# More pairs of half-wide products in the ConvFFN, none in the short convolution

## The chip, the cores and the metric

The kernel runs on one core of one Trainium2 chip. The metric is the device time of one execution in microseconds; before the change the median of three runs is 1096.01 us (1095.03 to 1096.32).

## The reference

A trunk of two layers on 512 positions of 1024 channels, all in float32. Layer 0 mixes positions by gated linear attention in chunks of 64 with 4 heads, layer 1 by a short gated convolution; each mixer is followed by a causal ConvFFN, and each of the four blocks reads an RMS norm of x and adds its result to x. A last norm ends it.

```
x = x + mixer(rmsnorm(x))                   # layer 0: GLA;  layer 1: y = b * conv3(c * u), then y @ w_out
up = conv3(rmsnorm(x) @ w_up)               # causal, depthwise, width 3; 2 x 2816 columns
a, u = up[..., :2816], up[..., 2816:]
x = x + (silu(a) * u) @ w_down
```

## The kernel before, in words

**Layout and precision.** Channels lie on the 128 partitions and the 512 positions on the free axis, so x is 8 tiles x[0..7] of 128 x 512. Every float32 product is made of three matmuls: each operand is split into a high half in the format that TensorE multiplies and a low half with the remainder, and high x high, high x low and low x high are added up in PSUM (`mm3`, L282). The norm's gain goes into these halves of x (`norm_parts`, L307 and L308), its row factor r is multiplied in after the product.

**Weights.** All weights are read once, as a list of units of up to 128 x 1024, in the order in which they are used (class `Weights`). A unit is loaded on SyncE's queue into one of 6 raw buffers, then split into halves in one of 4 buffers (L127 on ScalarE for the high half). The low half comes from VectorE (L132: raw minus high), or, for a unit that is marked `added`, from ScalarE, which writes the negated high half (L129), and a DMA on GpSimd's queue that adds the raw values to it (L130). `take()` hands out one unit and prepares the third unit after it. Before the change only the units of w_down are marked.

**ConvFFN.** It has 22 columns of 128 channels; column j has an a tile and a u tile, two units of w_up. They are worked through in four blocks of 6, 5, 5 and 6 columns; between the columns of a block stand the down products (`dn`) of the block before, which add into x. `ff_steps` writes this order out. A column of the plain kind is a step `up`: two groups of 24 matmuls with 512 columns. A column in `SEVEN` is a pair of the other kind: the two tiles, the two halves of the 8 channel tiles and the two halves of the positions make a 2 x 2 by 2 x 2 block product, which is done with seven half-size products instead of eight (`product`, L605; 12 matmuls of 256 columns each), in steps `s1` (four products) and `s2` (three). For it the raw weights of the two tiles are added and subtracted on VectorE (`forms`, L141 to L148), and the x parts likewise once per ConvFFN (`seven_forms`, L589 to L595): four sets, k = 0..3, each from x[k] and x[k + 4], made after columns 1 to 4. The results are joined by quarter-size operations (L626 to L642), and then every column goes through the convolution, silu, the gating product and a split into halves g (L297, L298).

**Short convolution.** Eight times three whole groups (c, u and b, 24 matmuls each), a convolution between, then 8 groups `so` that add into x.

**Order.** The program text gives priorities; a scheduler at compile time places each instruction on its engine's queue by when it expects it to be ready, and the queues run in that order. The row norm's sum of squares (L318, L319) is split (L324, L325) between the first and the second group after a residual and summed on TensorE after the second (`inv_rms_rows`).

Of the kernel before, what the change touches and what calls it, by code (L numbers as in the profile page):

```python
# [10 lines left out]
F32 = mybir.dt.float32  # L11
F32R = mybir.dt.float32r
AF = mybir.ActivationFunctionType
ALU = mybir.AluOpType
# [13 lines left out]
WARM = 10  # L28
BLOCKS = ((0, 6), (6, 11), (11, 16), (16, 22))
HALVED = 4  # L30
SEVEN = (6, 7, 8, 9, 10, 11, 12, 13, 14, 15, 16, 17, 18, 20, 21)


@with_exitstack
def trunk_kernel(ctx, tc, xT, w_qk, w_v, w_g, w_up_gate, b_gate, w_go, w_sc, w_so, w_up, w_dn,
# [15 lines left out]
    def wk(name, shape=(P, T), dt=F32, bufs=2, tag=None, pool=work):  # L51
        return pool.tile(list(shape), dt, tag=tag or name, name=name, bufs=bufs)
# [141 lines left out]
            return self.split.pop(self.ng - 1)  # L194

    W = Weights()
    for src in ([w_qk[i] for i in range(8)] + [w_v[i] for i in range(8)] + [w_g[i] for i in range(8)]
                + [w_go[i] for i in range(8)]):
# [24 lines left out]

    add_ffn(0)
    for src in [w_sc[i] for i in range(3 * KD)] + [w_so[i] for i in range(KD)]:
        W.add(src)
    add_ffn(1)
    take = W.take

# [336 lines left out]
    gate_tile(6)  # L566
    gate_tile(7)

    def residual(src, gi):
        for m in range(KD):  # L570
            V.tensor_add(x[m], x[m], src(m))
            norm_parts(m, gi)
            norm_squares(m)


    go, w = [ps("go0"), ps("go1")], [take(), take()]
# [3 lines left out]
                mm3(go[m], w[m][k], yparts[k], k == 0, k == KD - 1)  # L580
    residual(lambda m: go[m] if m < 2 else group(f"go{m}", yparts), 1)


    def seven_forms(k, gi, y, neg):


        lo, hi = slice(0, HT), slice(HT, T)
        g1, g2 = col(gi, k), col(gi, k + 4)
        S.activation(y[:, lo], x[k][:, hi], AF.Copy, scale=g1)  # L589
        S.activation(y[:, hi], x[k + 4][:, hi], AF.Copy, scale=g2)  # L590
        ta, tb = wk("ta", tag="sq"), wk("tb", tag="sq")
        V.scalar_tensor_tensor(ta[:, lo], x[k][:, lo], g1, y[:, lo], op0=ALU.mult, op1=ALU.subtract)
        V.tensor_sub(tb[:, lo], y[:, lo], y[:, hi])
# [4 lines left out]
        return [tuple(p[:, c] for p in t) for t in (a, b) for c in (lo, hi)]  # L598

    def product(out, ws, xs, first):  # L600
        for k in range(4):
# [12 lines left out]
    def cut(ks, c):  # L614
        return [tuple(p[:, c] for p in xparts[k]) for k in ks]

    def seven_first(tf):
# [5 lines left out]
        us = [wk("u", bufs=3) for _ in range(2)]  # L623
# [6 lines left out]
        S.copy(us[0][:, lo], ab[:, hi])  # L630
        V.tensor_add(us[0][:, lo], us[0][:, lo], ab[:, lo])
        return dc, ab, e, us

    def seven_last(dc, ab, e, us, tf):
# [4 lines left out]
        S.copy(us[0][:, hi], ab[:, lo])  # L639
        V.tensor_sub(us[1][:, lo], dc[:, lo], us[0][:, hi])  # L640
        V.tensor_sub(us[1][:, hi], e, us[0][:, hi])
        V.tensor_add(us[0][:, hi], dc[:, hi], us[0][:, hi])  # L642
        return us

    def ffn_blocks(l, gi, gnext):
        gp, r, tf = {}, None, [[], [], [], []]
        neg = tk("neg", (P, KD), bufs=1)
        V.tensor_scalar_mul(neg, vec[:, gi * KD:(gi + 1) * KD], -1.0)
        for st in ff_steps():
            if st[0] == "dn":  # L650
                _, b, m = st
                if gnext is None and b == len(BLOCKS) - 1 and m == HALVED:
                    break
                part = group(f"dn{m}", [gp[j] for j in range(*BLOCKS[b])])
                V.tensor_add(x[m], x[m], part)  # L655
                if b == len(BLOCKS) - 1:
                    if gnext is not None:
                        norm_parts(m, gnext)
                    norm_squares(m)
                continue  # L660
            j = st[1]
            if st[0] == "s1":
                begun = seven_first(tf)
                continue
            if st[0] == "s2":
                us = seven_last(*begun, tf)
                for u in us:
                    V.tensor_mul(u, u, r)  # L668
            else:
                ups = [group("up0", xparts)]  # L670
                if j == 0:
                    sums = sum_parts(acc[0])
                ups.append(group("up1", xparts))
                if j == 0:
                    r = inv_rms_rows(sums, D)
                    y = wk("y", tag="acc", bufs=1)
                us = [wk("u", bufs=3) for _ in range(2)]
                for u, up in zip(us, ups):
                    V.tensor_mul(u, up, r)
            cs = [conv3(us[i], ffcw[:, l, i * NFF + j, :], f"c{i}") for i in range(2)]  # L680
            S.activation(cs[0], cs[0], AF.Silu)  # L681
            V.tensor_mul(cs[1], cs[1], cs[0])
            gp[j] = split_to(cs[1], f"g{j}", f"b{j % 11}")
            if len(SEVEN) and 1 <= j <= 4:
                for t, f in zip(tf, seven_forms(j - 1, gi, y, neg)):
                    t.append(f)
        return [gp[j] for j in range(*BLOCKS[-1])]

    HT = T // 2
    ffn_blocks(0, 1, 2)  # L690


    yparts = []
    for i in range(KD):
        cp = group("scc", xparts)
        if i == 0:
            sums = sum_parts(acc[0])
        up = group("scu", xparts)
        if i == 0:
            r = inv_rms_rows(sums, D)  # L700
        cr = wk("u", bufs=3)
        V.tensor_mul(cr, cp, r)
        ur = wk("u", bufs=3)
        V.tensor_mul(ur, up, r)
        V.tensor_mul(ur, ur, cr)
        cv = conv3(ur, sccw[:, i, :], "c0")
        V.tensor_mul(cv, cv, r)
        bp = group("scb", xparts)
# [5 lines left out]
    gp = ffn_blocks(1, 3, None)  # L714

    wlast = {m: take() for m in range(HALVED, KD)}

# [133 lines left out]
```

## Time and profile before

| | |
|---|---|
| profiled execution | 1095.35 us |
| its span, first to last instruction | 1093.6 us |
| median of three runs | 1096.01 us |
| granted TensorE clock, mean over the span | 0.997 |
| ScalarE busy | 593.1 us, 54% |
| GpSimd busy | 60.4 us, 6% |
| chain that ended last | TensorE 98%, DMA 1% |

A busy time is the time in which an engine executes something. Matmuls are pipelined, so one may be counted as running while the next has begun, and the mean duration of one is longer than the distance from its start to the start of the next. The chain of waits is followed back from the last instruction, at each step to what released it or to the instruction before it on its engine; in order of time it reads as the path that sets the end.

### The profile page before, as it was taken

The page shows a single profiled execution, that of the slowest core. Times are in us where ns is not written, and L with a number is a line of the kernel's source. Part 1 is how long each engine was busy: PE and PEld are TensorE (multiplying, and loading weights), DVE is VectorE, ACT ScalarE, POOL GpSimd, SP SyncE. Part 2 cuts the span into 40 slices and gives each one's busy share as a digit, 9 for nine tenths or more (in the row PEclk, how much of TensorE's full clock was granted, in tenths as well). Part 3 has the DMA queues.
Part 4 walks back from the last instruction along what each step waited for, and adds up shares of the span by engine and source line. Part 5 has one row for each costly group of instructions (what it writes and reads, how often), then busy time and mean ns, then how long its engine had stood idle before and what let it go on. Part 6 is the DMA issues. An engine that isn't in the chain of part 4 may idle for free.

```text
span 1093.6 us, 15686 instructions
## 1 busy us (share of the span) xinstructions
PE 1083.8 (99%) x6106; PEld 953.0 (87%) x6106; DVE 842.9 (77%) x1267; ACT 593.1 (54%) x902; POOL 60.4 (6%) x82
## 2 busy tenths in 40 slices
PE   9999999999999999999999999999999999999997
PEld 7888888888999999989888888888899999999986
DVE  8874676589889899897566555568988989899754
ACT  7565764466555565556642222345655655655563
POOL 1000000000000000001200000000000000000020
PEclk9999999999999999999999999999999999999998
DMA  8332123321545545355853333332254654545473
GB/s 290 109 93 81 58 78 97 96 92 54 150 126 145 138 133 137 107 150 125 204 170 92 102 89 104 97 100 68 82 140 108 161 139 121 139 126 150 116 149 93
DMA packets 44719, 131.42 MB, mean 120 GB/s; under 512 B 4898, under 2 KB 7714, under 8 KB 44644
## 3 DMA queue, kind: packets, MB, share of 16 engines
q1 hardware_dynamic: 35428, 107.34, 31.3%
q0 software_dynamic: 9216, 23.07, 11.7%
q8 instruction: 47, 0.77, 0.3%
q14 instruction: 28, 0.23, 0.1%
HBM read 105.23 MB, written 2.10 MB: 98 GB/s over the span
## 4 chain that ended last, share of the span: by engine, by line
PE 98%; DMA 1%; ACT 0%; DVE 0%; issue 0%; SPq 0%; DVEq 0%
PE dn L282 21%; PE updc L605 16%; PE up L282 14%; PE upab L605 12%; PE g L282 4%; PE v L282 4%; PE so L282 4%; PE scb L282 4%; PE scu L282 4%; PE scc L282 4%; PE go L282 4%; PE k L282 2%; PE q L282 2%; PE dnl L282 1%; PE o L504 1%; PE o L506 0%
## 5 line engine op out<-in xcount | busy, mean ns | idle before, releaser
L127 ACT CAST wh<-wr 128x1024 fp32r<-128x1024 f32 (+4 forms) x280 | 247.0, 884 | 339.7 <-PE upab L605 78.7
L132 DVE TENSOR_TENSOR wl<-wr,wh 128x1024 fp32r<-128x1024 f32 (+2 forms) x216 | 225.6, 1052 | 67.9 <-ACT wh L127 67.5
L130 POOL DMA_DIRECT2D wl<-wr x64 | 55.4, 866 | 977.2 <-ACT wl L129 725.7
L282 PE MATMUL up<-xh,wh 128*128 128x512 f32 x224 | 87.1, 389 | 0.0
L282 PE MATMUL up<-xl,wh 128*128 128x512 f32 x224 | 87.1, 389 | 0.0
L282 PE MATMUL up<-xh,wl 128*128 128x512 f32 x224 | 87.1, 389 | 0.0
L341 ACT ACTIVATE c<-u,ffcw 128x512 f32<-128x512 f32 x88 | 59.8, 716 | 32.2 <-DVE u L668 19.2
L605 PE MATMUL upab<-xh,wh 128*128 128x256 f32 x240 | 67.9, 283 | 0.0
L605 PE MATMUL upab<-xl,wh 128*128 128x256 f32 x240 | 67.9, 283 | 0.0
L605 PE MATMUL upab<-xh,wl 128*128 128x256 f32 x240 | 67.9, 283 | 0.0
L342 DVE SCALAR_TENSOR_TENSOR c<-u,ffcw,c 128x511 f32<-128x511 f32 x88 | 62.8, 745 | 6.0 <-ACT c L341 6.0
L343 DVE SCALAR_TENSOR_TENSOR c<-u,ffcw,c 128x510 f32<-128x510 f32 x88 | 62.6, 743 | 0.1
L129 ACT ACTIVATE wl<-wh 128x768 fp32r<-128x768 f32 (+1 forms) x64 | 50.8, 794 | 0.9
L282 PEld LDWEIGHTS up<-xh,wl 128*128 128x128 f32 x224 | 42.0, 188 | 8.8
L282 PEld LDWEIGHTS up<-xh,wh 128*128 128x128 f32 x224 | 42.0, 188 | 8.8
L282 PEld LDWEIGHTS up<-xl,wh 128*128 128x128 f32 x224 | 42.0, 188 | 8.6
L655 DVE TENSOR_TENSOR x<-x,dn 128x512 f32<-128x512 f32 x60 | 40.9, 682 | 10.8 <-PE dn L282 10.4
L605 PEld LDWEIGHTS upab<-xh,wh 128*128 128x128 f32 x240 | 46.1, 192 | 0.0
L605 PEld LDWEIGHTS upab<-xl,wh 128*128 128x128 f32 x240 | 46.1, 192 | 0.0
L605 PEld LDWEIGHTS upab<-xh,wl 128*128 128x128 f32 x240 | 46.1, 192 | 0.0
L681 ACT ACTIVATE c<-c 128x512 f32<-128x512 f32 x44 | 27.8, 632 | 29.9 <-DVE c L343 29.9
L668 DVE TENSOR_TENSOR u<-u,r 128x512 f32<-128x512 f32 x60 | 38.5, 683 | 0.0
(682 smaller groups left out, 3210.3 us busy)
## 6 DMA issues: line engine op xcount, KB each, us to landing
wr<-in_w_up SPq DMA_DIRECT2D x88, 512.0 KB, 3.6
wr<-in_w_dn SPq DMA_DIRECT2D x32, 384.0 KB, 3.4
wl<-wr POOLq DMA_DIRECT2D x32, 384.0 KB, 4.4
wr<-in_w_sc SPq DMA_DIRECT2D x24, 512.0 KB, 3.6
wr<-in_w_dn SPq DMA_DIRECT2D x32, 320.0 KB, 2.9
wl<-wr POOLq DMA_DIRECT2D x32, 320.0 KB, 3.8
wr<-in_w_v SPq DMA_DIRECT2D x8, 512.0 KB, 3.6
wr<-in_w_g SPq DMA_DIRECT2D x8, 512.0 KB, 3.7
```

Source lines behind the costliest of these rows:

```text
L127: S.copy(hh, src)
L129: S.activation(ll, hh.bitcast(F32), AF.Copy, scale=-1.0)
L130: G.dma_start(ll, src, accum_op=ALU.add)
L132: V.tensor_sub(ll, src, hh.bitcast(F32))
L282: PE.matmul(out, lhsT=a, rhs=b, start=first and i == 0, stop=last and i == 2)
L341: S.activation(c, u, AF.Copy, scale=cw[:, 2:3])
L342: V.scalar_tensor_tensor(c[:, 1:], u[:, :T - 1], cw[:, 1:2], c[:, 1:], op0=ALU.mult, op1=ALU.add)
L343: V.scalar_tensor_tensor(c[:, 2:], u[:, :T - 2], cw[:, 0:1], c[:, 2:], op0=ALU.mult, op1=ALU.add)
L605: PE.matmul(out, lhsT=a, rhs=b, start=first and k == 0 and i == 0, stop=k == 3 and i == 2, skip_group_check=not first)
L655: V.tensor_add(x[m], x[m], part)
L668: V.tensor_mul(u, u, r)
L681: S.activation(cs[0], cs[0], AF.Silu)
```

## The change

- The list `SEVEN` goes. In both ConvFFNs the columns 3, 5 and 6 to 21 are pairs of the other kind; 0, 1, 2 and 4 stay whole. Block 0 runs as up 0, up 1, s1 3, first tile of 2 (`ua`), s2 3, s1 5, second tile of 2 (`ub`), s2 5, up 4.
- The sets of x parts are made in the residual before a block (`settle`): k = 0 with x[5], k = 1 with x[6], k = 2 and 3 with x[7]; also in the one before the short convolution. They have temporary buffers of their own (tags b12h, b12l, b13l).
- More units are marked `added`: the whole units of w_up, all of w_sc, and the second half of w_go and w_so. So are the halves of gated tiles except columns 4, 10, 15, 20 and 21 (`SOON`) and of the first six y parts of the short convolution.
- The short convolution could take pairs of c and u (`SC_SEVEN`); that list is empty, so all its groups stay whole. It multiplies c by the square of r instead of c and u by r each.
- `seven_first` and `seven_last` allocate the second result tile later.

```diff
-SEVEN = (6, 7, 8, 9, 10, 11, 12, 13, 14, 15, 16, 17, 18, 20, 21)
+SOON = (4, 10, 15, 20, 21)
+SC_SEVEN = ()
...
+    for m in range(KD):
+        W.add(w_go[m], m >= KD // 2)
...
-        steps = [("up", j) for j in range(*BLOCKS[0])]
+        steps = [("up", 0), ("up", 1), ("s1", 3), ("ua", 2), ("s2", 3), ("s1", 5), ("ub", 2), ("s2", 5), ("up", 4)]
...
-                steps += [("s1", j), dn[0], ("s2", j)] + dn[1:] if j in SEVEN else [("up", j)] + dn
+                steps += [("s1", j), dn[0], ("s2", j)] + dn[1:]
...
-                W.add(w_up[l, 2 * st[1]])
-                W.add(w_up[l, 2 * st[1] + 1])
+                for i in {"up": (0, 1), "ua": (0,), "ub": (1,)}[st[0]]:
+                    W.add(w_up[l, 2 * st[1] + i], True)
...
-    def split_to(src, name, tag):
+    def split_to(src, name, tag, added=False):
...
-        S.copy(h, src)
-        V.tensor_sub(l, src, h.bitcast(F32))
+        W.halve(h, l, src, added)
...
-        ta, tb = wk("ta", tag="sq"), wk("tb", tag="sq")
+        ta, tb = bt("b12h", f"ta{gi}{k}"), bt("b12l", f"tb{gi}{k}")
...
+    def settle(m, part, gi):
+
+        V.tensor_add(x[m], x[m], part)
+        norm_parts(m, gi)
+        norm_squares(m)
+        if m == 0:
+            settle.neg, settle.y = tk("neg", (P, KD), bufs=1), bt("b13l", f"y{gi}")
+            V.tensor_scalar_mul(settle.neg, vec[:, gi * KD:(gi + 1) * KD], -1.0)
+            for t in tf:
+                del t[:]
+        for k in {5: (0,), 6: (1,), 7: (2, 3)}.get(m, ()):
+            for t, f in zip(tf, seven_forms(k, gi, settle.y, settle.neg)):
+                t.append(f)
...
+        def gate(j):
+            a, u = cs.pop((j, 0)), cs.pop((j, 1))
+            S.activation(a, a, AF.Silu)
+            V.tensor_mul(u, u, a)
+            gp[j] = split_to(u, f"g{j}", f"b{j % 11}", j not in SOON)
...
+                r2 = bt("b10h", "r2s")
+                V.tensor_mul(r2, r, r)
+            cr, ur = wk("u", bufs=3), wk("u", bufs=3)
+            V.tensor_mul(cr, cp, r2)
+            V.tensor_mul(ur, up, cr)
...
-        yparts.append(split_to(cv, f"s{i}", f"b{i}"))
+        yparts.append(split_to(cv, f"s{i}", f"b{i}", i < KD - 2))
```

## Rows read from the trace of the kernel before

**Rows 1.** The page's busy shares: engine, us, share of the span, instructions.
```profile
PE 1083.8 (99%) x6106; PEld 953.0 (87%) x6106; DVE 842.9 (77%) x1267; ACT 593.1 (54%) x902; POOL 60.4 (6%) x82
```

**Rows 2.** The chain of waits in order of time: start us, length us, what.
```profile
210.82 10.88 PE up L282 x48
...
276.55 2.87 PE updc L605 x24
279.42 2.88 PE upab L605 x24
282.30 4.11 PE dn L282 x18
286.41 2.87 PE updc L605 x24
289.28 1.44 PE upab L605 x12
```

**Rows 3.** The costliest groups of TensorE: count, busy us, mean ns, idle before.
```profile
L282 PE MATMUL up<-xh,wh 128*128 128x512 f32 x224 | 87.1, 389 | 0.0
...
L605 PE MATMUL upab<-xh,wh 128*128 128x256 f32 x240 | 67.9, 283 | 0.0
```

**Rows 4.** Busy us by stage, layer 0: ConvFFN block 0, block 2, block 3.
```profile
210.65:276.55 65.90, 65.90 (x293) 54.59 (x292) 59.53 (x89) 40.79 (x60) 1.01 (x1) 1.00 0.25 74
359.75:437.51 77.76, 77.76 (x542) 72.90 (x542) 71.17 (x118) 45.36 (x76) 6.89 (x8) 1.00 0.51 137
437.51:526.10 88.59, 88.59 (x589) 81.88 (x589) 73.16 (x118) 50.92 (x82) 8.63 (x10) 1.00 0.52 135
```
Columns after the stretch: its length, TensorE, its weight loads, VectorE, ScalarE, GpSimd, granted clock, DMA share, GB/s.

**Rows 5.** Groups of instructions by shape on VectorE and ScalarE.
```profile
L132 DVE TENSOR_TENSOR wl<-wr,wh 128x1024 fp32r<-128x1024 f32 x150 | 182.9, 1220 | 64.4 <-ACT wh L127 64.1
L132 DVE TENSOR_TENSOR wl<-wr,wh 128x512 fp32r<-128x512 f32 x62 | 42.4, 685 | 2.8 <-ACT wh L127 2.8
L592 DVE SCALAR_TENSOR_TENSOR ta<-x,small,y 128x256 f32<-128x256 f32 x8 | 3.8, 475 | 6.5 <-PE sums L332 6.5
...
L127 ACT CAST wh<-wr 128x1024 fp32r<-128x1024 f32 x150 | 157.3, 1049 | 242.2 <-issue 49.3 <-PE upab L605 41.5 <-PE scu L282 32.1
L127 ACT CAST wh<-wr 128x512 fp32r<-128x512 f32 x62 | 38.2, 619 | 12.4 <-DVE wr L143 5.1 <-DMA wr<-in_w_up 4.5 <-PE updc L605 2.5
L129 ACT ACTIVATE wl<-wh 128x768 fp32r<-128x768 f32 x32 | 27.1, 847 | 0.5
```

**Rows 6.** The page's DMA issues, accumulating ones: count, KB each, us to landing.
```profile
wl<-wr POOLq DMA_DIRECT2D x32, 384.0 KB, 4.4
...
wl<-wr POOLq DMA_DIRECT2D x32, 320.0 KB, 3.8
```

**Rows 7.** The page's DMA queues: packets, MB, share of 16 engines over the span.
```profile
q1 hardware_dynamic: 35428, 107.34, 31.3%
q0 software_dynamic: 9216, 23.07, 11.7%
```

**Rows 8.** DMA queues and issues from 526 to 559 us, block 3's down products.
```profile
q1 hardware_dynamic: 1323, 4.72, 41.0%
q0 software_dynamic: 864, 2.36, 38.7%
...
wl<-wr POOLq DMA_DIRECT2D x5, 384.0 KB, 5.6
```

**Rows 9.** Order of time on ScalarE and GpSimd, there: start, length, instruction.
```profile
539.20 0.85 ACT L129 ACTIVATE wl<-wh 128x768 fp32r<-128x768 f32 x1
...
538.80 0.86 POOL L130 DMA_DIRECT2D wl<-wr  x1 [2.89 <-ACT wl L129]
540.40 0.88 POOL L130 DMA_DIRECT2D wl<-wr  x1 [0.73 <-ACT wl L129]
```

**Rows 10.** VectorE after the last group of w_go: low half of the squares.
```profile
214.89 0.69 DVE L325 TENSOR_TENSOR sl<-acc,sh 128x512 fp32r<-128x512 f32 x1 [0.69 <-ACT sh L324]
```

More of the change, by code (lines that the diff above doesn't have):

```diff
@@ L196, in trunk_kernel @@
     W = Weights()
-    for src in ([w_qk[i] for i in range(8)] + [w_v[i] for i in range(8)] + [w_g[i] for i in range(8)]
-                + [w_go[i] for i in range(8)]):
+    for src in [w_qk[i] for i in range(8)] + [w_v[i] for i in range(8)] + [w_g[i] for i in range(8)]:
         W.add(src)
+    for m in range(KD):
+        W.add(w_go[m], m >= KD // 2)
     def ff_steps():
-        steps = [("up", j) for j in range(*BLOCKS[0])]
+        steps = [("up", 0), ("up", 1), ("s1", 3), ("ua", 2), ("s2", 3), ("s1", 5), ("ub", 2), ("s2", 5), ("up", 4)]
         for b in range(1, len(BLOCKS)):
@@ L220, in add_ffn @@
             else:
-                W.add(w_up[l, 2 * st[1]])
-                W.add(w_up[l, 2 * st[1] + 1])
+                for i in {"up": (0, 1), "ua": (0,), "ub": (1,)}[st[0]]:
+                    W.add(w_up[l, 2 * st[1] + i], True)
     add_ffn(0)
-    for src in [w_sc[i] for i in range(3 * KD)] + [w_so[i] for i in range(KD)]:
-        W.add(src)
+    for i in range(KD):
+        c, u, b = (w_sc[3 * i + n] for n in range(3))
+        if i in SC_SEVEN:
+            pair = W.add_pair(c, u)
+            W.add(b, True)
+            W.end_pair(pair)
+        else:
+            for src in (c, u, b):
+                W.add(src, True)
+    for m in range(KD):
+        W.add(w_so[m], m >= KD // 2)
     add_ffn(1)
@@ L567, in trunk_kernel @@
     gate_tile(7)
[L569 to L576, printed above, removed]
-    for ks in (range(0, 6), range(6, 8)):
-        for m in range(2):
-            for k in ks:
-                mm3(go[m], w[m][k], yparts[k], k == 0, k == KD - 1)
-    residual(lambda m: go[m] if m < 2 else group(f"go{m}", yparts), 1)
+    HT = T // 2
+    tf = [[], [], [], []]
     def seven_forms(k, gi, y, neg):
@@ L598, in seven_forms, with residual @@
         return [tuple(p[:, c] for p in t) for t in (a, b) for c in (lo, hi)]
+    def settle(m, part, gi):
[10 more added lines that the diff above has]
+                t.append(f)
+    def residual(src, gi):
+        for m in range(KD):
+            settle(m, src(m), gi)
+    go, w = [ps("go0"), ps("go1")], [take(), take()]
+    for ks in (range(0, 6), range(6, 8)):
+        for m in range(2):
+            for k in ks:
+                mm3(go[m], w[m][k], yparts[k], k == 0, k == KD - 1)
+    residual(lambda m: go[m] if m < 2 else group(f"go{m}", yparts), 1)
     def product(out, ws, xs, first):
@@ L629, in seven_first, with seven_last @@
         product(ab[:, hi], w2, cut(range(4, 8), lo), False)
[L630 to L634, printed above, removed]
+        u = wk("u", bufs=3)
+        S.copy(u[:, lo], ab[:, hi])
+        V.tensor_add(u[:, lo], u[:, lo], ab[:, lo])
+        return dc, ab, e, u
+    def seven_last(dc, ab, e, u):
         product(dc[:, lo], halves(take())[0], tf[3], False)
@@ L638, in seven_last, with ffn_blocks, conv @@
         product(ab[:, lo], w2, tf[1], False)
[L639 to L648, printed above, removed]
+        u1 = wk("u", bufs=3)
+        S.copy(u[:, hi], ab[:, lo])
+        V.tensor_sub(u1[:, lo], dc[:, lo], u[:, hi])
+        V.tensor_sub(u1[:, hi], e, u[:, hi])
+        V.tensor_add(u[:, hi], dc[:, hi], u[:, hi])
+        return u, u1
+    def ffn_blocks(l, gnext):
+        gp, cs, r = {}, {}, None
+        def conv(j, i, u, src):
+            V.tensor_mul(u, src, r)
+            cs[j, i] = conv3(u, ffcw[:, l, i * NFF + j, :], f"c{i}")
+        def gate(j):
[3 more added lines that the diff above has]
+            gp[j] = split_to(u, f"g{j}", f"b{j % 11}", j not in SOON)
         for st in ff_steps():
@@ L651, in ffn_blocks @@
                 _, b, m = st
-                if gnext is None and b == len(BLOCKS) - 1 and m == HALVED:
+                last = b == len(BLOCKS) - 1
+                if gnext is None and last and m == HALVED:
                     break
                 part = group(f"dn{m}", [gp[j] for j in range(*BLOCKS[b])])
[L655 to L659, printed above, removed]
@@ L660, in ffn_blocks @@
-                continue
[L661 to L668, printed above, removed]
-            else:
[L670 to L673, printed above, removed]
+                if last and gnext is not None:
+                    settle(m, part, gnext)
+                else:
+                    V.tensor_add(x[m], x[m], part)
+                    if last:
+                        norm_squares(m)
@@ new lines, in ffn_blocks @@
+                continue
+            step, j = st
+            if step == "s1":
+                begun = seven_first()
+            elif step == "s2":
+                for i, u in enumerate(seven_last(*begun)):
+                    conv(j, i, u, u)
+                gate(j)
+            else:
+                tiles = {"up": (0, 1), "ua": (0,), "ub": (1,)}[step]
+                ups = {}
+                for i in tiles:
+                    ups[i] = group(f"up{i}", xparts)
+                    if j == 0 and i == 0:
+                        sums = sum_parts(acc[0])
@@ L684, in ffn_blocks @@
-            if len(SEVEN) and 1 <= j <= 4:
-                for t, f in zip(tf, seven_forms(j - 1, gi, y, neg)):
-                    t.append(f)
+                for i in tiles:
+                    conv(j, i, wk("u", bufs=3), ups[i])
+                if 1 in tiles:
+                    gate(j)
         return [gp[j] for j in range(*BLOCKS[-1])]
-    HT = T // 2
-    ffn_blocks(0, 1, 2)
+    ffn_blocks(0, 2)
     yparts = []
     for i in range(KD):
[L695 to L705, printed above, removed]
+        if i in SC_SEVEN:
+            begun = seven_first()
+            bp = group("scb", xparts)
+            cr, ur = seven_last(*begun)
+            V.tensor_mul(cr, cr, r2)
+            V.tensor_mul(ur, ur, cr)
+        else:
+            cp = group("scc", xparts)
+            if i == 0:
+                sums = sum_parts(acc[0])
+            up = group("scu", xparts)
+            if i == 0:
+                r = inv_rms_rows(sums, D)
+                r2 = bt("b10h", "r2s")
[3 more added lines that the diff above has]
+            V.tensor_mul(ur, up, cr)
+            bp = group("scb", xparts)
@@ L706, in trunk_kernel @@
         cv = conv3(ur, sccw[:, i, :], "c0")
         V.tensor_mul(cv, cv, r)
-        bp = group("scb", xparts)
         V.tensor_mul(cv, cv, bp)
-        yparts.append(split_to(cv, f"s{i}", f"b{i}"))
+        yparts.append(split_to(cv, f"s{i}", f"b{i}", i < KD - 2))
     residual(lambda m: group(f"so{m}", yparts), 3)
-    gp = ffn_blocks(1, 3, None)
+    gp = ffn_blocks(1, None)
     wlast = {m: take() for m in range(HALVED, KD)}
```

11 lines of the change are left out of this document (1 added, 10 removed).

## The prediction

> **What bounds the kernel now.** I read the busy shares first: TensorE is busy 99% of the span, VectorE 77% [rows 1]. A busy matrix engine can still hide waits, so I went to the chain of waits in order of time [rows 2]. The reader is to see that one TensorE piece starts where the one before ends: 210.82 plus 10.88 is 221.70, 276.55 plus 2.87 is 279.42. It goes on like that through all stages; the kernel is a queue of matmuls with no gap to close. So the time moves by what TensorE's list of work gains or loses, or by a wait that opens where there is none today. The table by stages [rows 4] says how near the helpers are to opening one: VectorE is busy 71.17 of 77.76 us (92%) in block 2, still without a gap in TensorE's work.
>
> **TensorE: three more pairs per layer, six in all.** Columns 3, 5 and 19 of each ConvFFN go from two whole products to seven half-wide ones (before: 15 of 22 columns, after: 18). A whole pair is 2 groups of 24 matmuls of 512 columns: 48 in 10.88 us, 226.7 ns each. A pair of the other kind is 84 matmuls of 256 columns in four pieces: 2.87 + 2.88 + 2.87 + 1.44 = 10.06 us, 119.8 ns each [rows 2]. The mean durations of one matmul, 389 and 283 ns [rows 3], must not be used here: they overlap, and 84 x 283 against 48 x 389 would make the seven products the dearer ones. From start to start the saving is 10.88 - 10.06 = 0.82 us a pair, and 6 x 0.82 = **4.9 us**. It is an eighth of the columns, yet only 7.5% of the time, because the narrower matmul spends 119.8 ns and not half of 226.7. The gated short convolution keeps its 24 whole groups, and nothing else in the diff changes a matmul.
>
> The Trainium skill (TensorE: Matmul & The Clock Gate, "Back-to-back issue gap") speaks against this: it gives a stream of weight load and matmul about 81 ns at 128 columns and 131 ns at 512. On the straight line between, about 98 ns at 256, an estimate, seven products would take 84 x 98 = 8.2 us and the whole pair 48 x 131 = 6.3 us, so the change would add 6 x 1.9 = 11.7 us. The trace of this kernel does not agree: 226.7 and 119.8 ns.
>
> **VectorE.** Per new pair it gets the sums of the weights and their halves: four operations of 512 columns (0.685 us each [rows 5]), then 1.22 + 2 x 0.685, then 0.685, then 1.22, together 7.2 us against 2 x 1.22 = 2.4 for two whole units; and five operations of 256 columns, at most 0.475 us each, to join the products: 9.6 against 2.4, +7.2 us a pair. It loses the low halves that now go through ScalarE's negation and an accumulating DMA: 0.685 us for 17 of the 22 gated tiles of a layer, 1.22 us for each of the 8 remaining whole units of w_up, all 24 of w_sc, and half of w_go and w_so. By stage, with busy times from [rows 4]:
> - Block 3: 73.16 + 7.2 (pair 19) - 4 x 0.685 = 77.6 us, in 88.59 - 0.82 = 87.8 us: 88%.
> - Block 2: 71.17 - 4 x 0.685 = 68.4 of 77.76 us: 88%, below today's 92%.
> - Block 0: 59.53 less four sets of prepared x parts (4 x 0.475 + 2 x 0.685 = 3.3 us each, moved ahead into the residual), less 12 x 1.22 for whole units, less 5 x 0.685, plus 2 x 9.6 for pairs 3 and 5: 47.5 of 64.3 us, 74%.
> So VectorE is below the share that it carries today without a gap, and I cost it at nothing. If that cover were gone, block 3 alone would pay what lies above 100%; the sum of all its work would have to be 13% larger than I count.
>
> **The x parts, moved.** They are now made when x[5], x[6] and x[7] are finished (the last two sets after x[7]), in three places: before up 0 of both layers, and before the short convolution, where nothing uses them. Queued near them is the sum of squares that the row norm needs: its low half ends at 215.58 today [rows 10], 4.8 us after the last group (the next pieces start at 210.82 [rows 2]), and TensorE wants it two groups later, after 10.9 us. So 6.1 us are free there. The two last sets hold VectorE for 2 x 3.3 = 6.5 us, but their steps alternate with ScalarE's copies, so the sum can slip in between. Between nothing and rival 2's price I take nothing, the nearer end, since the free 6.1 us are about what VectorE puts in front.
>
> **The accumulating DMAs.** They go from 64 to 152: 16 more for w_up, 32 for w_go, w_so and w_sc (4 + 4 + 24), 34 for gated tiles and 6 for y parts of the short convolution. A whole unit's low half then takes: copy 1.05, negation about 1.05 (0.85 at 768 columns, an estimate by the copy's slope [rows 5]), 0.35 to the issue (ScalarE's negation ends at 540.05, GpSimd issues at 540.40 [rows 9]), and a landing of about 5.6 us (estimate: 3.8 at 320 KB and 4.4 at 384 KB [rows 6], 0.6 more per 64 KB): 8.1 us. In the stage that is densest today 384 KB take 5.6 us [rows 8], 1.2 more, so 9.3 us. Units are prepared three ahead, 3 x 5.44 = 16.3 us in whole stages: covered. It is tight at one unit only, the second w_up tile of column 2 between the halves of pair 5. Its buffer is free when the first tile of column 2 is done, and it is wanted 1.44 + 2.87 + 2.87 + 2.88 = 10.06 us later: 0.8 to 2.0 us of room, with ScalarE shared. I take 0.3 us in all here, and rival 1 has the rest. The Trainium skill (DMA: Bandwidth & Descriptors, "Anatomy of one DMA — SWDGE (gpsimd) path") has 2.0 us plus the bytes at 436 GB/s, an estimated 3.2 us for 512 KB, by which rival 1 would fall away; the trace does not agree, at 3.8 us for 320 KB.
>
> Load of the short convolution: the 64 transfers of the software queue took 11.7% of 1093.6 us for 23.07 MB, 5.5 us per MB; the other queue 3.2 us per MB [rows 7]. A unit of 0.524 MB loaded and accumulated is 1.7 + 2.9 us, the y parts 0.4 more per unit: 5.0 of 5.44 us, 91% of the DMA engines. Today's densest stage holds 41.0 + 38.7 = 80% [rows 8] and TensorE does not stop.
>
> **The sum.** The profiled execution took 1095.35 us: a span of 1093.6 and 1.75 around it. 1095.35 - 4.9 + 0.3 = 1090.7. The median of the runs, 1096.01, lies 0.66 above that execution, so **1091.4 us**, 0.4% faster. The likeliest case by itself is 1090.5 to 1092.6.
>
> **Rivals.**
> 1. Short waits at the head of both ConvFFNs. For: the 0.8 to 2.0 us of room above; and block 0's last gated tile, which TensorE takes 5.75 us and two thirds of a group (of 4.11 us) after its column. Against: in both places TensorE needs the low half as the last of three terms. 0.75 to 2 us per layer: +1.5 to +4, 1092.9 to 1095.4.
> 2. ScalarE's queue at the residuals. If both last sets and the next unit's copy and negation stand ahead of the sum of squares, ScalarE has, with 0.62 us at 512 columns and 0.40 at 256 (an estimate by the slope from 1024 to 512 [rows 5]), 1.24 + 2 x 2.04 + 2.1 + 0.62 = 8.0 us, and waits twice 1.9 us for VectorE: with an addition before and a subtraction after it 13.2 us, 2.3 over the 10.9. At the short convolution, where a group before it is 4.11 us and not 5.44 [rows 2], each of sets 0 and 1 adds 2.1 + 1.24 + 2.04 - 4.11 = 1.3 us: 2 x 2.3 + 4.9 = 9.5 us, 1100.9. It decides from the point where that low half comes later than 10.9 us. Against: this is the worst of many orders, and ScalarE is idle in the waits that it counts.
> 3. The short convolution becomes bound by its transfers. If accumulations go one after the other, each takes issue to landing, 5.6 + 0.35 us or more against 5.44 of TensorE: 0.5 x 24 = 13 us, 1104. For: 91% by my count. Against: GpSimd issues 1.6 us apart (538.80, 540.40 [rows 9]) while landings take 5.6, so several are under way.
> 4. The narrower matmul is no cheaper. From a spacing of 129.5 ns (10.88 / 84) on, the seven products lose; at 226.7 ns, no cheaper at all, they cost 19.0 - 10.9 = 8.2 us more a pair, 49 in all, 1145. Against: 119.8 ns in today's pairs. By the rule on the clock gate page of the Trainium skill, above, it would be 1107.7.
>
> **Chances.** Forecast 0.66, rival 1 0.14, rival 2 0.09, rival 3 0.08, rival 4 0.01, other 0.02. What a measurement of this kernel can tell from no change is 0.2%, 2.2 us: faster means under 1093.8, slower over 1098.2. Rival 1 gives 0.06 to faster and 0.08 to same; rival 2 in its weaker form (one place, 2.3 to 4.9 us) gives 0.04 to same, and the rest to slower; other counts as faster. Faster 0.74, same 0.12, slower 0.14. Range 1090.2 to 1097.5: the forecast, rival 1 and the weak form of rival 2, 0.84; its low end is the sum without the 0.3 (1091.1) less 0.9, about what the fastest run of before lies under their median.
>
> **What would show it.** 36 pairs of four pieces with 119.8 ns spacing; whole pairs still 10.88 us; no TensorE gap at the sums of squares, at the second tile of column 2, or between groups of the short convolution; VectorE below 92% in blocks 1 to 3; DMA share near 0.9 in the short convolution. I am wrong if TensorE's busy time falls by other than 4.9 us, or if the span falls by less than its busy time.

## The result and the profile after

The changed kernel takes 1102.73 us (median of 4 runs, 1101.49 to 1103.71) against 1095.62 us before: ratio 1.0065, 95% interval 1.0049 to 1.0081. It is slower by 7.1 us; the forecast was 4.6 us faster. The profiled execution took 1103.71 us, its span 1102.0. In the experiments below, one run of e4 (1538.02 us) and one of e12 (2181.90 us) were slow, and the times given are medians of the other runs.

The busy shares and the DMA rows of the page, after (answering to rows 1, 6 and 7):

```profile
PE 1083.1 (98%) x6322; PEld 960.1 (87%) x6322; DVE 809.6 (73%) x1269; ACT 678.6 (62%) x1042; POOL 136.6 (12%) x170
...
q1 hardware_dynamic: 35428, 107.34, 30.6%
q0 software_dynamic: 21888, 58.73, 29.4%
...
wl<-wr POOLq DMA_DIRECT2D x48, 512.0 KB, 5.7
...
wl<-wr POOLq DMA_DIRECT2D x32, 384.0 KB, 4.4
...
wl<-wr POOLq DMA_DIRECT2D x32, 320.0 KB, 4.1
```

Against [rows 1], VectorE lost 33 us and ScalarE gained 85. A low half of 512 KB takes 5.7 us (median) from issue to landing, as estimated (5.6). TensorE's busy time fell by 0.7 us, from 1083.8 to 1083.1, and not by 4.9: the prediction had named this as a sign of being wrong. A busy time also grows where the clock is low (one matmul of 512 columns then counts 0.63 us instead of 0.39), so what the pairs save is read from start to start.

The chain of waits in order of time, in block 0 of layer 0, after (answering to rows 2):

```profile
242.02 5.47 PE up L294 x24
247.49 2.87 PE updc L631 x24
250.36 1.44 PE upab L631 x12
251.80 2.89 PE updc L631 x24
```

These are the first tile of column 2, the second half of pair 3, and the first product of pair 5. The new pairs cost what the old ones did, and no gap stands between the pieces.

The table by stages, after: block 0 (up to its last plain column), 2 and 3 of layer 0, and most of the short convolution (columns as in rows 4):

```profile
210.52:278.08 67.56, 64.78 (x363) 56.49 (x362) 59.76 (x95) 48.09 (x72) 9.11 (x11) 1.00 0.63 155
362.05:439.81 77.76, 77.76 (x543) 72.91 (x542) 69.34 (x114) 47.66 (x80) 10.38 (x12) 1.00 0.59 150
439.81:527.58 87.77, 87.77 (x626) 82.92 (x625) 75.90 (x125) 55.13 (x92) 12.16 (x14) 1.00 0.58 147
560.00:735.00 175.00, 175.00 (x773) 144.95 (x773) 73.25 (x109) 92.96 (x119) 29.50 (x34) 1.00 0.83 193
```

Blocks 2 and 3 run without a gap and VectorE is at 89% and 86%, near the 88% of the forecast. The short convolution has no gap either, at a DMA share of 0.83 (forecast 0.91). Block 0 is another matter: TensorE is busy 64.78 of 67.56 us, and VectorE at 88% where 74% was forecast.

What TensorE waits for, after (total us, times, longest; `wr` is a raw buffer, `wh` and `wl` the halves of a unit, `xh` and `xl` those of x, `g4h` and `g4l` those of column 4's gated tile):

```profile
PE up L294 <- ACT xh L318: 3.9, 2, 2.5
PE dn L294 <- ACT g4h L128: 2.1, 1, 2.1
...
PE dn L294 <- DMA wl<-wr: 1.5, 2, 0.9
PE dn L294 <- DVE g4l L133: 1.0, 2, 0.7
...
PE up L294 <- DVE xl L319: 0.6, 2, 0.3
```

All of these are new; the rows left out, for the first matmuls and the last sums, stood there before the change as well. Adding up the distances from start to start beyond the usual 226.7 and 119.8 ns gives, in us: before up 0 3.3 in layer 0 and 3.8 in layer 1, at the end of block 0 (its last gated tile, g4) 0.6 and 4.2, at two places of block 3 in layer 1 1.5. Together 13.4. The forecast's sum for TensorE, 1095.35 - 4.92, leaves 13.3 us to explain, so these waits are the whole difference.

The same execution before up 0 of layer 0. First the chain of waits in order of time (start us, length us, what):

```profile
199.30 4.54 DMA wr<-in_w_up
```

Then VectorE's queue by order of time (start, length, instruction, in brackets the idle time before it and what ended it):

```profile
203.93 0.69 DVE L142 TENSOR_TENSOR s<-wr,wr 128x512 f32<-128x512 f32 x1 [4.71 <-DMA wr<-in_w_up]
...
205.14 0.68 DVE L601 TENSOR_TENSOR x<-x,go 128x512 f32<-128x512 f32 x1
...
220.57 0.69 DVE L336 TENSOR_TENSOR sl<-acc,sh 128x512 fp32r<-128x512 f32 x1
```

And ScalarE's, the same columns:

```profile
217.17 0.72 ACT L318 ACTIVATE xh<-x,small 128x512 fp32r<-128x512 f32 x1
```

VectorE stands for 4.71 us at L142, the sum of the raw weights of pair 3, whose load lands at 203.83. Behind it in the queue wait the addition to x[5] (205.14), then the chains of x[6] and x[7]; x[7]'s high half comes at 217.17, when TensorE has been through the other seven tiles. Pair 3 itself is multiplied only from 236.26. The weights are not late for their consumer, only for the place that their sum has in VectorE's queue. The Trainium skill (PSUM — Partial Sum Buffer, "Engine vs sequencer instructions") calls the queues of ScalarE, VectorE and GpSimd "strict FIFO". These rows agree: the addition at 205.14 stands behind the sum at 203.93.

Why did the load come late? The raw buffer that it fills belonged to a unit of w_go. ScalarE began to copy that unit at 188.74, and GpSimd issued its accumulating transfer here (columns as for VectorE):

```profile
192.18 0.86 POOL L131 DMA_DIRECT2D wl<-wr  x1 [4.58 <-ACT wl L130]
```

This transfer landed 7.1 us after its issue, at 199.3, and the load starts at 199.30. The same stands in the chain of waits at the end of block 0, before the sum of pair 6's weights (start us, length us, what):

```profile
257.23 5.02 DMA wl<-wr
262.25 0.02 SPq L122
262.27 0.03 issue
262.30 5.39 DMA wr<-in_w_up
```

What SyncE's queue waits for in the whole execution (total us, times, longest), before the change:

```profile
SPq L121 <- DMA wl<-wr: 284.3, 58, 7.9
```

And after it:

```profile
SPq L122 <- DMA wl<-wr: 557.4, 106, 14.0
```

In 106 places a load now waits for an accumulating transfer to land, since that transfer still reads the raw buffer that the load wants to fill. The number alone is no price: in e3 below 82 loads wait in this way, 401.0 us in all, and TensorE waits for none of them.

Part of the 13.4 us is the clock. Two stretches around up 0 of layer 1 (columns as in rows 4):

```profile
739.30:742.80 3.50, 1.84 (x6) 0.93 (x5) 3.40 (x8) 3.50 (x6) 0.00 (x0) 0.96 0.66 131
742.80:745.80 3.00, 3.00 (x9) 2.35 (x8) 2.96 (x6) 2.70 (x6) 0.87 (x1) 0.50 0.67 208
```

After a stretch in which TensorE was busy 1.84 of 3.50 us, the granted clock is 0.50 (1.2 GHz) in the next 3 us: seven matmuls 427 ns apart, 1.4 us lost beside the wait. They are part of the 3.8 us.

### The profile page after: what moved, and what is told of

It is laid out like the page before. It is cut to its first block, busy times and chain, and to the rows that moved or that the text cites. A ratio compares the mean times of both kernels' runs of the same rounds, so it can differ in the third digit from the quotient of the medians.

```text
span 1102.0 us, 16587 instructions
## 1 busy us (share of the span) xinstructions
PE 1083.1 (98%) x6322; PEld 960.1 (87%) x6322; DVE 809.6 (73%) x1269; ACT 678.6 (62%) x1042; POOL 136.6 (12%) x170
## 4 chain that ended last, share of the span: by engine, by line
PE 65%; issue 16%; DVE 7%; DMA 6%; ACT 3%; POOL 2%; SPq 0%; POOLq 0%; DVEq 0%; ACTq 0%
PE updc L631 16%; PE dn L294 16%; PE upab L631 12%; PE g L294 4%; PE v L294 4%; DMA wr<-in_w_up 4%; PE up L294 3%; PE go L294 2%; PE k L294 2%; PE q L294 2%; POOL wl L131 2%; DMA wl<-wr 2%; PE dnl L294 2%; DVE wl L133 1%; DVE c L353 1%
## 5 line engine op out<-in xcount | busy, mean ns | idle before, releaser
L133 DVE TENSOR_TENSOR wl<-wr,wh 128x1024 fp32r<-128x1024 f32 (+2 forms) x180 | 174.5, 983 | 52.0 <-ACT wh L128 51.3
L131 POOL DMA_DIRECT2D wl<-wr x112 | 97.9, 874 | 694.6 <-ACT wl L130 358.0
L130 ACT ACTIVATE wl<-wh 128x1024 fp32r<-128x1024 f32 (+2 forms) x112 | 101.1, 903 | 1.1
L294 PE MATMUL up<-xh,wh 128*128 128x512 f32 x128 | 50.8, 397 | 3.9 <-ACT xh L318 3.9
L294 PE MATMUL up<-xl,wh 128*128 128x512 f32 x128 | 50.9, 397 | 0.6 <-DVE xl L319 0.6
L294 PE MATMUL up<-xh,wl 128*128 128x512 f32 x128 | 50.4, 394 | 0.0
L142 DVE TENSOR_TENSOR s<-wr,wr 128x512 f32<-128x512 f32 x36 | 24.8, 688 | 27.5 <-DMA wr<-in_w_up 26.0
L631 PE MATMUL updc<-xh,wh 128*128 128x256 f32 x144 | 40.8, 283 | 0.0
L631 PE MATMUL updc<-xl,wh 128*128 128x256 f32 x144 | 40.8, 283 | 0.0
L631 PE MATMUL updc<-xh,wl 128*128 128x256 f32 x144 | 40.8, 283 | 0.0
```

Source lines behind the costliest of these rows:

```text
L130: S.activation(ll, hh.bitcast(F32), AF.Copy, scale=-1.0)
L131: G.dma_start(ll, src, accum_op=ALU.add)
L133: V.tensor_sub(ll, src, hh.bitcast(F32))
L142: V.tensor_add(s3, ra[:, lo], rb[:, lo])
L294: PE.matmul(out, lhsT=a, rhs=b, start=first and i == 0, stop=last and i == 2)
L631: PE.matmul(out, lhsT=a, rhs=b, start=first and k == 0 and i == 0, stop=k == 3 and i == 2, skip_group_check=not first)
```

## The experiments

In the expectations, theory A says that the accumulating transfers make the weights late because they hold the raw buffers; D that it is ScalarE's load of negations; E that the order of VectorE's and ScalarE's queues, made at compile time, lets a load that is a little late block work that is wanted sooner. F joins A and E, G is its rival. Each kernel is the changed one but for its diff; e2, e3, e6, e7, e8 and e10 say from which they start.

**e1, e2, e3: which transfers.**

```diff
 e1, e3, in w_go and in w_so:
-        W.add(w_go[m], m >= KD // 2)
+        W.add(w_go[m])
 e2, e3, whole columns of w_up:
-                    W.add(w_up[l, 2 * st[1] + i], True)
+                    W.add(w_up[l, 2 * st[1] + i])
```

> The second half of w_go and w_so gets its low halves from VectorE again, all else as changed. Theory A (raw buffers): an accumulating transfer holds its raw buffer until it lands, so the load of pair 3's weights comes late, VectorE's sum for that pair stands at the head of its queue and keeps x[6] and x[7] waiting. Then the two waits of TensorE before up 0 (3.3 and 3.8 us) go: 1102.7 - 7.1 = 1095.6 us. Theory B (load): the four sets of x parts are too much for ScalarE and VectorE in the residual. Then the waits stay or grow, since VectorE has 1.22 us more per group: 1102.5 to 1105 us.

> The eight whole units of w_up per ConvFFN get their low halves from VectorE again. Theory A: the waits before up 0 stay (their raw buffers are those of w_go and w_so), the waits at the end of block 0 (0.6 us in layer 0, 4.2 in layer 1) fall under 1 us in all: 1098 to 1099.5 us. Theory C (the end of block 0 is late because pairs 3 and 5 stand close together and share 6 raw buffers, whoever makes the low halves): nothing falls, VectorE has 9.8 us more in block 0: 1102 to 1104 us.

> Both at once: w_go, w_so and the whole units of w_up from VectorE, w_sc and the gated tiles still by accumulating transfers. Theory A for both places: only the saving of TensorE is left, 1091 to 1093 us. Theory B at the residuals: 1098 us or more. Theory C at the end of block 0: 1094.5 to 1096.5 us.

e1: 1098.28 us, ratio 1.0025 (1.0015 to 1.0034), 2.7 us more than theory A expected and far below B. The waits before up 0 are gone; the end of block 0 in layer 1 stays and costs more, 6.3 us from start to start where it was 4.2. Of these 6.3, some 1.5 are a granted clock of 0.50 for 3.4 us from 810.02, which the changed kernel does not have there:

```profile
PE dn L294 <- ACT g4h L128: 2.1, 1, 2.1
...
PE dn L294 <- DMA wl<-wr: 1.3, 1, 1.3
```

e2: 1094.72 us, 0.9993 (0.9984 to 1.0002), below what either theory expected. The end of block 0 is clean, and these waits stand before up 0 (from start to start 3.7 us in layer 0, with 1.6 of low clock in them, and 0.7 in layer 1):

```profile
PE up L294 <- DVE xl L319: 1.4, 2, 0.9
PE up L294 <- ACT xh L318: 0.6, 1, 0.6
```

e3: **1090.53 us**, 0.9953 (0.9939 to 0.9968). TensorE waits for nothing that it did not wait for before the change, and its busy time is 4.4 us below that of before:

```profile
PE 1079.4 (99%) x6322; PEld 960.0 (88%) x6322; DVE 834.1 (77%) x1293; ACT 656.3 (60%) x1018; POOL 115.9 (11%) x146
```

VectorE's sum of pair 3's weights comes 9.3 us earlier than in the changed kernel:

```profile
194.65 0.69 DVE L142 TENSOR_TENSOR s<-wr,wr 128x512 f32<-128x512 f32 x1 [2.34 <-DMA wr<-in_w_up]
```

VectorE stands there for 2.34 us here too, but early enough that TensorE misses nothing. So the pairs are worth the forecast 4.9 us (1095.53 before in this series, 5.0 less), and 24 transfers too many (16 of w_up, 8 of w_go and w_so) cost 12.2 us. The two groups of transfers feed different places in the main, but not one each: e2 also took most of the wait before up 0 of layer 1 away (0.7 us left of 3.8). e3 beats both kernels, with the transfers of w_sc and of the tiles kept.

**e4: block 0 with six whole columns, every transfer kept** (`steps = [("up", j) for j in range(*BLOCKS[0])]`, and column 5 for 4 in `SOON`).

> Block 0 in the order of before, six whole columns, 16 pairs per ConvFFN in place of 18; the sets of x parts stay in the residuals and all accumulating transfers stay. Theory A: no sum of a pair's weights stands in VectorE's queue at the residual, so the waits before up 0 and at the end of block 0 go, and TensorE has 4 x 0.82 = 3.3 us more than in the changed kernel: 1093.5 to 1095 us. Theory B: the waits before up 0 stay, 7 us: 1100 to 1102 us.

1107.29 us, 1.0115 (1.0098 to 1.0132), a miss for both theories. Two pairs of the other kind fewer in each layer cost some 3.3 us; the waits before up 0 are gone, as theory A said, but those at the end of block 0 now stand at the weights of the first down product, and grew:

```profile
PE dn L294 <- DMA wl<-wr: 10.4, 2, 5.4
```

GpSimd's queue there, by order of time:

```profile
283.25 0.86 POOL L131 DMA_DIRECT2D g4l<-c  x1 [11.30 <-ACT g4l L130]
284.12 0.88 POOL L131 DMA_DIRECT2D wl<-wr  x1
```

The transfer that the down product's weights need is issued behind g4's, and the chain of waits runs back from there to VectorE's sum of pair 6 at 269.66, where it stood for 4.84 us. A third engine's queue passes the delay on.

**e5, e7: one raw buffer more, or one less.** e5 has seven buffers (some small tiles share memory to make room); e7 starts from e3 and has five.

```diff
-    wraw = ctx.enter_context(tc.tile_pool(name="wraw", bufs=6))
+    wraw = ctx.enter_context(tc.tile_pool(name="wraw", bufs=7))
...
-                if self.nl < len(self.srcs) and (self.nl < 6 or self.last[self.nl - 6] < self.ns):
+                if self.nl < len(self.srcs) and (self.nl < 7 or self.last[self.nl - 7] < self.ns):
```

> The changed kernel with 7 raw weight buffers in place of 6 (and loads that run one unit further ahead); all 152 accumulating transfers and all negations stay. Room is made by sharing small buffers (row factor of the heads, joining quarter, ones). Theory A (a low half made by a transfer holds its raw buffer until it lands, some 6 us longer, about one unit of 5.44 us): one more buffer takes that back, most of the 13 us of waits go, 1091 to 1095 us. Theory D (ScalarE's negations, 1.05 us for each unit of w_go, w_so and w_up, stand in front of the high half of x[7] and of the gated tiles): the waits stay, 1100 to 1104 us.

> The kernel without transfers for w_go, w_so and w_up (1090.5 us), with 5 raw weight buffers in place of 6 and loads that run one unit less ahead. Theory A: waits of the same kind come back without any of those transfers, at the first sum of a pair's weights: 1093 to 1102 us. Theory D: the number of raw buffers does not matter, 1090.5 to 1091.5 us.

e5: 1104.37 us, 1.0079 (1.0064 to 1.0095): theory A's number fell. The end of block 0 is clean, but the waits before up 0 have doubled (8.5 us for xh where 3.9 stood). The sum of pair 3's weights is not what holds x[7] here: it stands at 196.63, and x[7] is added up by 214.40, earlier than in the changed kernel. The compiler had put a copy of raw weights ahead of the last x parts on ScalarE, and x[7]'s high half comes behind it, at 219.28:

```profile
217.72 0.62 ACT L129 CAST wh<-wr 128x512 fp32r<-128x512 f32 x1 [4.41 <-DMA wr<-in_w_up]
```

By the chain of waits the load of these weights starts at 212.68, when an accumulating transfer has landed (6.02 us from 206.61). So the raw buffers are held by transfers with seven of them too; what the seventh changed is which load is waited for.

e7: 1098.4 us, 1.0025 (1.0013 to 1.0037). Without any of the 24 transfers, loads that start one buffer later bring waits back, at g4 and g15 and not before up 0:

```profile
PE dn L294 <- DVE g4l L133: 1.7, 1, 1.7
...
PE dn L294 <- DVE g15l L133: 1.5, 2, 0.8
PE dn L294 <- ACT g4h L128: 0.9, 1, 0.9
```

So raw buffers that come free too late are enough; the transfers are one way to get there.

**e6: e3 with the negations that the 24 transfers would need, written to their low halves and then overwritten by VectorE. e8: only w_down by transfers, as before the change.**

```diff
 e6, in halve, for those units:
+                if idle:
+                    S.activation(ll, hh.bitcast(F32), AF.Copy, scale=-1.0)
 e8, from e3:
-                W.add(src, True)
+                W.add(src)
...
-            gp[j] = split_to(u, f"g{j}", f"b{j % 11}", j not in SOON)
+            gp[j] = split_to(u, f"g{j}", f"b{j % 11}", False)
...
-        yparts.append(split_to(cv, f"s{i}", f"b{i}", i < KD - 2))
+        yparts.append(split_to(cv, f"s{i}", f"b{i}", False))
```

> The kernel without transfers for w_go, w_so and w_up (1090.5 us), but with ScalarE's negation of each of those units back in its queue, overwritten at once by VectorE's subtraction: the load on ScalarE without the transfer. Theory A: 1090.5 to 1092 us. Theory D: the waits come back, 1096 us or more.

> The three pairs more per layer and the x parts in the residuals, but accumulating transfers for w_down alone, as before the change (w_go, w_so, w_up, w_sc, gated tiles and y parts all by VectorE). If VectorE needed no relief, as its 92% in block 2 without a wait says: 1090.3 to 1091.5 us, the same as without transfers for w_go, w_so and w_up. If it did (block 3 with pair 19 comes to 73.2 + 7.2 = 80.4 of 87.8 us, 92%): 1092 to 1096 us, with TensorE waits in blocks 1 to 3.

e6: 1090.36 us, 0.9952 (0.9937 to 0.9967), as e3 though ScalarE is as busy (678.9 us) as in the changed kernel: theory D falls. e8: 1091.97 us, 0.9971 (0.9961 to 0.9981), between the two ranges expected, with one short wait at g4 (0.6 us) and none in blocks 1 to 3. So the transfers of gated tiles, w_sc and y parts are worth about 1.6 us (against e6 of the same series), of which the trace shows 0.8, at g4; the rest of the gain is the pairs'.

**e9, e10, e11: the order of the queues.** The sums of pair 3's weights (VectorE) and the copies of them (ScalarE) are queued behind the halves of x[7]; no transfer changes. e10 is this on e2. e11 does the like for pair 6 as well, behind column 2's gating product.

```diff
+                        if pair[1] < 2:
+                            for ins in self.behind.get(self.first.get(pair[0]), ()):
+                                st.enter_context(tc.issue_after(ins))
                         self.forms(pair[0], pair[1], h, l)
```

> As the kernel after, every transfer kept. Only the place of a few instructions in two queues changes: in both ConvFFNs the sums of the weights of the first pair (column 3) on VectorE, and the copies of them on ScalarE, are queued behind the halves of x[7] instead of some 15 us ahead of them. Theory E (the order of the queues: VectorE stands for 4.5 us at weights that nobody needs yet, and what stands behind is wanted by TensorE): the waits before up 0 of both layers go, 3.3 + 3.8 us, the end of block 0 in layer 1 stays: 1102.7 - 7.1 = 1095.6 us (1094.5 to 1097). Theory A (the accumulating transfers make the weights themselves too late): the pair's parts come later still, and TensorE waits at column 3 for them what it no longer waits before up 0, or more: 1101 or more.

> The kernel of e2 (the whole columns of w_up as before, w_go, w_so, w_sc, gated tiles and y parts by accumulating transfers), with the first pair of both ConvFFNs queued behind the halves of x[7] as in e9. E2 has 4.2 us of waits left, all before up 0. Theory E: they go, 1094.7 - 4.2 = 1090.5 us (1090 to 1091.5), the sum of the prediction without a wait, with 16 fewer transfers than after. Theory A: the accumulations of w_go and w_so still hold the raw buffers: no change from e2, 1094 or more.

> As e9, and in both layers the first pair of block 1 (column 6) is queued on VectorE and ScalarE behind column 2's gating product, instead of ahead of its convolution. Theory E: the blocked 4.4 us of VectorE (5.3 of ScalarE) at the end of block 0 in layer 1 become harmless in part, since other work still stands behind: of 4.2 us of waits there 2 to 4 go, 1095.6 - 3 = 1092.6 us (1091.4 to 1094). Theory A: as e9 expects by A, 1101 or more; if only the start of block 0 is a matter of order and its end is one of late loads, 1095.6 as e9.

e9: 1103.07 us, 1.0076 (1.0058 to 1.0094). The waits before up 0 are gone in both layers, as E said, and the time is the same, as E did not say; it is in A's range, but TensorE does not wait at column 3, as A had it. Pair 3's sum now stands at 216.60 with no wait before it, and all is paid later: 0.6 us at the second tile of column 2 in layer 0, and the rest at the end of block 0, now in both layers (4.9 and 5.8 us from start to start):

```profile
PE dn L300 <- ACT g4h L129: 4.2, 2, 2.1
```

The chain there:

```profile
258.99 4.45 DMA wl<-wr
...
263.49 5.83 DMA wr<-in_w_up
```

Transfer, release of the raw buffer, load, and then VectorE's sum of pair 6 at 269.42, from which VectorE works without a pause until g4's low half at 288.18. That moment hardly moved: the first down product ended at 288.71 in the changed kernel and at 290.86 here, and 1.5 of these 2.2 us are older than the block (up 0 began at 212.07, not 210.52). By these chains it is set by the loads, not by when TensorE began the block. Part of what is paid is the clock, in both layers (columns as in rows 4; the second such stretch begins at 815.25), some 1.6 us each:

```profile
289.60:293.01 3.41, 3.41 (x16) 3.11 (x15) 2.92 (x5) 1.68 (x2) 0.47 (x1) 0.50 0.00 0
```

e11: 1104.78 us, 1.0082 (1.0067 to 1.0097), a miss for E, in A's range: with pair 6's sum behind column 2 the end of block 0 costs 7.7 us in layer 0 (4.9 in e9) and 5.1 in layer 1 (5.8). e10: 1093.08 us, 0.9972 (0.9961 to 0.9983), 1.6 us less than e2 where 4.2 were expected, and between the two theories; 0.9 us stayed before up 0, and 1.7 came back, 0.5 at g4 and 1.2 in block 3 of layer 1 (beside g11 at a low half of w_down, and where the products of a pair are joined).

**e12, e13, e14: free the raw buffers early.** In e12 the accumulating transfers of weights read the raw values a second time from the device's memory. Their number, the negations and GpSimd's queue stay, but the raw buffer is free once ScalarE has copied it. e14 is e12 with e9's order, e13 is e5 with e9's order.

```diff
-                G.dma_start(ll, src, accum_op=ALU.add)
+                G.dma_start(ll, src if again is None else again, accum_op=ALU.add)
...
-                    self.halve(hh, ll, r[:, c:e], self.ns in self.added)
+                    self.halve(hh, ll, r[:, c:e], self.ns in self.added, self.srcs[self.need[self.ns]][:, c:e])
```

> As the kernel after, with one edit: the accumulating transfers of the weights read the raw values a second time from the device's memory instead of from the raw buffer. The count of transfers, ScalarE's negations and GpSimd's queue stay; the raw buffer is free as soon as ScalarE has copied the high half. Theory F (the raw buffers held until the landing make the loads late; the queues' order only says where this is paid): the waits go, 1090.5 to 1093 us. Rival G (the landing of the low halves or the engines' extra work): the waits stay or grow, since the transfers now also load the device's memory: 1100 us or more. Theory E (order alone): the order is made at compile time from expected times and changes as well, so it gives no number here.

> Seven raw buffers as in e5, and the first pair of both ConvFFNs queued behind the halves of x[7] as in e9. Alone, e5 took the waits at the end of block 0 away and e9 those before up 0, each paid with waits at the other place. Theory F: one more buffer gives the chain of loads about 5.4 us of lead, the order holds the waits off up 0: 1091 to 1094 us. Rival G: the waits move to one of the two places as before: 1100 us or more.

> e12 and e9 together. Theory F: as e12 or up to 2 us less, 1090.3 to 1092 us, since nothing late is left for the order to move. Rival G: as e12, 1100 us or more.

e12: 1094.77 us, 0.9993 (0.9983 to 1.0003): 8.0 of the 12.2 us between the changed kernel and e3 are back with all 152 transfers in place. That is 1.8 us above F's range, and far from G's. What SyncE's queue waits for most in e12:

```profile
SPq L122 <- DVE wl L133: 321.7, 67, 9.9
SPq L122 <- ACT wh L128: 317.2, 75, 7.5
```

And the landings, from its page:

```profile
wl<-in_w_dn POOLq DMA_DIRECT2D x32, 384.0 KB, 5.5
...
wl<-in_w_up POOLq DMA_DIRECT2D x16, 512.0 KB, 5.6
```

No load waits for a transfer any more, though the transfers land no sooner. e14: 1093.25 us, 0.9982 (0.9972 to 0.9991), 1.5 us less and 1.3 above F's range; the order is worth something once the loads are early. What is left there:

```profile
PE dn L300 <- DMA wl<-in_w_dn: 1.0, 1, 1.0
PE up L300 <- ACT xh L324: 0.8, 1, 0.8
```

The first of these is this edit's own: w_down's halves land 5.5 us after their issue, 4.4 in the changed kernel. It is 1.3 us from start to start. The second, 1.6 us with the wait for the low half behind it, stands before up 0 of layer 0, where ScalarE has a copy of raw weights ahead of x[7]'s high half (215.61):

```profile
213.09 0.62 ACT L129 CAST wh<-wr 128x512 fp32r<-128x512 f32 x1 [1.44 <-DMA wr<-in_w_up]
```

e13: 1108.3 us, 1.0113 (1.0096 to 1.013), where F expected 1091 to 1094: a miss, and in G's range. With seven buffers a copy of raw weights stands at the same place as in e5, one that the edit does not hold back, and x[7]'s high half waits behind it on ScalarE:

```profile
218.94 0.62 ACT L130 CAST wh<-wr 128x512 fp32r<-128x512 f32 x1 [5.47 <-DMA wr<-in_w_up]
```

In the chain of waits its load starts at 213.76, when an accumulating transfer has landed (6.94 us from 206.76). So the number is G's and the chain is F's: a raw buffer held until the landing.

**What is shown and what is open.** Shown: with the other transfers kept, the waits need those of w_up, w_go and w_so (e3); in the rows of the changed kernel, e5, e9 and e13 the load that is waited for starts when such a transfer has landed; ScalarE's load is not it (e6); most of them go when the raw buffers come free early (e12), and some come without transfers when buffers come free late (e7). Shown as well: the order of the queues decides where the delay is paid (e9), and mending one place moves it (e9, e11, e13). Open: in e14 2.7 us of the 12.2 have not come back, 1.3 of them at the landing of w_down's halves and 1.6 before up 0, as shown above; and no experiment made the transfers themselves land sooner. Argued only: that the compiler counts with shorter landings than the chip's; its counts are in no trace.

## Why the prediction was wrong

- **TensorE, 4.9 us: right.** Pieces of 2.87, 2.88 and 1.44 us, and e3 and e6 land 5.0 and 4.8 us below before. The estimate from the Trainium skill (TensorE: Matmul & The Clock Gate, "Back-to-back issue gap") would have made the pairs 11.7 us dearer; these runs do not agree with it, at 226.7 and 119.8 ns from start to start.
- **The accumulating DMAs: the step that failed.** The prediction put it so: a low half takes 8.1 to 9.3 us, "Units are prepared three ahead, 3 x 5.44 = 16.3 us in whole stages: covered", and "I take 0.3 us in all here". The 8.1 us were right (landing 5.7), but I held them only against the moment when TensorE wants the low half. The same 8.1 us are also the time for which the raw buffer is taken, against copy and subtraction (1.05 + 1.22 us) before. The next load into that buffer starts later by the difference: the buffer that pair 3's load waited for was taken for 10.5 us (188.74 to 199.3), and the sum of pair 3's weights came at 203.93 where e3 has it at 194.65. Nothing in my sum had a row for this. In place of 0.3 stand 12.2 us (the changed kernel less e3).
- **VectorE at nothing: wrong in kind.** I asked if its share stays below 92%. In block 0 it is 59.8 us of 67.6, not 47.5 of 64.3: 6.5 us of the difference are the two sets of x parts made after x[7], which I had counted out of the block; the other 5.8 are not traced. But e3 has VectorE at 63.4 of 64.2 us there, and TensorE does not stop. What counts in an ordered queue is what it stands at and who stands behind, not its share.
- **The x parts, moved: the free time was no cover.** I let the sum of squares have 6.1 us to spare. Its low half came 5.7 us later than in [rows 10], at 220.57, inside that bound; what TensorE missed was x[7]'s high half, one step ahead of it, which I had not looked at.
- **Rival 1** named the right place, g4, with 0.75 to 2 us a layer; it was 0.6 and 4.2, and the second tile of column 2 did not wait in the changed kernel. **Rival 2** named up 0, for a full ScalarE; the place was right, the cause in the changed kernel was not (e6; only what is left in e14 runs through ScalarE's queue), and the short convolution lost nothing. **Rival 3** is false: no gap in 175 us at a DMA share of 0.83. **Rival 4** is false (119.8 ns). None held the mechanism, and the range ended at 1097.5 because of that.
- The estimate from the Trainium skill (DMA: Bandwidth & Descriptors, "Anatomy of one DMA — SWDGE (gpsimd) path"), 3.2 us for 512 KB, is not what these transfers took, 5.7; with it the buffers would have seemed even safer.

## What to carry to other kernels

When work moves from an engine to a transfer, count how long each buffer is held, not only when the result is there: the next load through that buffer starts later by the difference. Then look along the in-order queues for instructions that wait on that load and ask what stands behind them. And a wait that goes at one place without the time falling has been moved: the cause lies upstream, here in when the buffers come free.

## What was not expected of the hardware

Before up 0 of layer 1, 3.5 us with TensorE busy for 1.84 of them were followed by 3 us at a granted clock of 0.50, with matmuls 427 ns apart instead of 226.7: short waits can cost more than their length. They need not: after the waits before up 0 of layer 0, 3.3 us, the granted clock stayed at 1.00. And an accumulating transfer of 512 KB landed in 5.6 us (w_up) and 6.0 us (w_sc) when it read the device's memory and in 5.7 over all units when it read the core's own: little difference, while at 384 KB the source did count (5.5 and 4.4).
